# Order of causal masks, output evacuation and output tiles in a stick-breaking attention stage

## Chip, cores and metric

The kernel runs on 1 core of one Trainium2 chip. The metric is the device time of one execution in microseconds (us), median over several runs. The profile is of one further execution, recorded by the hardware.

## The reference

A trunk of two layers on a sequence of 512 tokens with 1024 features, in float32. Layer 0 mixes tokens with a gated linear recurrence, layer 1 with stick-breaking attention; each mixer is followed by a gated feed-forward block. The change lies in the attention of layer 1, 16 heads of width 64:

```
z = einsum(q, k) * scale                      # per head, scale = 1/8
mask = key_pos < q_pos
log_beta = log_sigmoid(z)
log_1m = where(mask, log_sigmoid(-z), 0)
suffix = cumsum(log_1m, reverse) - log_1m
wts = where(mask, exp(log_beta + suffix), 0)
out = einsum(wts, v);  x = x + out_all_heads @ w_out
```

## The kernel before

Scores are held transposed: 128 keys on the partitions, queries along the free dimension. There are four key tiles, kt = 0 to 3; only queries from the tile's own on count, so the tiles are 512, 384, 256 and 128 columns wide. One head takes three PSUM banks: kt 0 fills the first, kt 1 the second, kt 2 and 3 lie side by side in the third. Six banks hold two heads, so head h uses the banks of head h - 2. The other two banks take projections, outputs of heads and the first output tiles.

To keep float32 accuracy, every operand is split into a high and a low part (the names end in h and l); a product takes two or three matmuls. For a weight chunk of 128x1024 the high part is a cast on ScalarE (L306; on VectorE, L304, where `wh_dve` is set) and the low part a subtraction (L307) on VectorE or GpSimd (POOL).

The steps of a head h, with the lines of the profile:

- `s1(h)`: the score products (L1139 with the high part of q, L1140 with the low part), for kt 0 to 3, and the causal masks (L1142): a bf16 identity times a bf16 matrix of -1e30, added into the diagonal 128 columns. The mask of the first bank follows kt 0; those of the second and third bank follow kt 3 (the third is 256 columns wide, since it covers the diagonals of kt 2 and kt 3).
- `chain_a(h)`: for each bank, on ScalarE Abs (L1159), Exp (L1160) and Ln (L1161), on VectorE two softplus results (L1162, and L1163 as sph), on POOL the low part spl (L1164).
- `rsum(h)`: sums of the third bank on VectorE (L1172, L1175, L1177), called between the steps of `chain_b` of the head before.
- `s2(h)`: sixteen matmuls (L1196) that add the suffix sums into the score banks.
- `chain_b(h)`: for each bank, on ScalarE two exponentials (L1209 into awh, L1210 in place), on VectorE the low part of the weights, awl (L1211). After the last awl of head h its banks are free for `s1(h + 2)`.
- `s3(h)`: eight matmuls (L1222) with v. `s3_evac(h)`: a copy on ScalarE (L1235) and an addition on VectorE (L1236) that bring the head's output from PSUM to `o`. In the last heads (h >= 13) only one bank is left for `s3`, because another, `fill`, holds an output tile; so `s3` of the next head waits for `s3_evac` of the one before.

Beside these run the projections of q and k (`proj`, L352 to L354, evacuated by L1103, split by L1111, L1112 or L1124, L1125), three heads ahead, and from the sixth iteration on `osplit`, which splits finished pairs of heads (L1255, L1256) for the output projection. When the projections are used up, from iteration 13 on, `out_part(m, lo, hi)` fills TensorE's order with parts of the output tiles: the products of output tile m with the head pairs lo to hi - 1, three matmuls each. `out_split` splits the next output weight chunk ahead of time, with the cast on VectorE (L304). `out_add` (L1271) adds an output tile to x.

The order is written out by hand: the whole loop stands in `manual_schedule` for TensorE, ScalarE, VectorE and POOL, so each of these engines executes in program order and waits where an operand isn't ready. In iteration h the order is: first half of a projection (or an output part), `s1(h + 1)`, the first two banks of `chain_a(h + 1)`, `osplit`, the second half of the projection, the third bank of `chain_a(h + 1)`, `s3(h - 1)`, `s2(h)`, `chain_b(h)`, `out_split` (iterations 13 and 14), `s3_evac(h - 1)`.

Of the kernel before, what the change touches and what calls it, by code (L numbers as in the profile page):

```python
# [16 lines left out]
P = 128  # L17
# [23 lines left out]
def ts(i, n=P):  # L41
    return slice(i * n, (i + 1) * n)
# [128 lines left out]
class Kern:  # L171
# [858 lines left out]
    def attention(self):  # L1030
        nc, tc = self.nc, self.tc
        mm = nc.tensor.matmul
# [3 lines left out]
        with ExitStack() as cx:  # L1036
# [9 lines left out]
            idb = ap_.tile([P, P], BF16, name="idb")  # L1046
            msk = ap_.tile([P, 2 * P], BF16, name="msk")
# [17 lines left out]
            def mps():  # L1065
                self.mi += 1
                return mb[self.mi % len(mb)]
# [25 lines left out]
            def proj(t, part):  # L1093
                if part == 0:
                    self.pt = mps()
                    self.pw = self.chunk()
                wh, wl = self.pw
                for k in range(4 * part, 4 * part + 4):
                    self.mm3(self.pt, wh[:, ts(k)], wl[:, ts(k)], *self.u[k], k == 0, k == KT - 1)

            def proj_evac1(t):
                tt = self.tt = self.tmp()
                nc.vector.scalar_tensor_tensor(tt, self.pt, 1.0 if t % 2 else 0.125, self.rsB, ALU.mult, ALU.mult)  # L1103
# [24 lines left out]
            def zslot(h):  # L1128
                b = zb[3 * (h % 2):3 * (h % 2) + 3]
                return tuple(b[min(k, 2)][:, ZO[k]:ZO[k] + ZW[k]] for k in range(4)), b  # L1130

            def s1(h):
                hd = heads[h]
                zt, b = zslot(h)
                masks = {0: ((0, 0, P),), 3: ((1, 0, P), (2, P, 3 * P))}
                for kt in range(4):
                    qs = slice(QO[kt], S)
                    lk = hd["ks"][:, ts(kt)]
                    mm(zt[kt], lhsT=lk, rhs=hd["qh"][:, qs], start=kt < 3, stop=False, skip_group_check=True)  # L1139
                    mm(zt[kt], lhsT=lk, rhs=hd["ql"][:, qs], start=False, stop=False, skip_group_check=True)  # L1140
                    for i, lo, hi in masks.get(kt, ()):
                        mm(b[i][:, lo:hi], lhsT=idb, rhs=msk[:, :hi - lo], start=False, stop=True,  # L1142
                           skip_group_check=True)
                self.rel(hd["qh"], hd["ql"], hd["ks"])

            BR = (slice(0, 512), slice(0, 384), slice(128, 512))
# [68 lines left out]
            def s3(h):  # L1215
                hd = heads.pop(h)
                av = avs[h] = mps()
                for j, src in enumerate((hd["wh"], hd["wl"])):
                    for kt in range(4):
                        i, off = min(kt, 2), ZO[kt]  # L1220
                        w = ZW[kt]
                        mm(av[:, QO[kt]:QO[kt] + w], lhsT=vs[kt][h // 4][:, h % 4, :], rhs=src[i][:, off:off + w],  # L1222
                           start=kt == 0 and j == 0, stop=kt == 3 and j == 1, skip_group_check=True)
                self.rel(*hd["wh"], *hd["wl"])
                if h % 4 == 3:
                    self.rel(*(vs[t][h // 4] for t in range(NT)))
                if h % 2 == 0:
                    o[h // 2] = self.new("o")
# [3 lines left out]
            def s3_evac(h):  # L1232
                av = avs.pop(h)
                tt = self.tmp()
                nc.scalar.copy(tt[0:64], av[64:128])  # L1235
                nc.vector.tensor_tensor(o[h // 2][64 * (h % 2):64 * (h % 2) + 64], av[0:64], tt[0:64], ALU.add)  # L1236

            E = mybir.EngineType
            with tc.manual_schedule(engines={E.PE, E.Activation, E.DVE, E.Pool}):
                self.wl_dve = True  # L1240
                for t in range(3):
                    proj(t, 0)
                    if t == 2:
                        s1(0)
                        chain_a(0)
                        for i in range(3):
                            rsum(0, i)
                    proj(t, 1)
                    proj_evac1(t)
                    proj_evac2(t)  # L1250
                self.wl_dve = False
                def osplit(p):
                    oh, ol = ou[p] = self.new("oh", F32R, True), self.new("ol", F32R, True)
                    self.keep2 = max(0, self.keep2 - 2)
                    nc.scalar.copy(oh, o[p])  # L1255
                    nc.vector.tensor_tensor(ol, o[p], oh.bitcast(F32), ALU.subtract)  # L1256
                    self.rel(o[p])

                outs = {}

                def out_part(m, lo, hi, bank=None, stop=KT):
                    if m not in outs:
                        outs[m] = [None, *self.chunk(1 if m < 3 else None), 0]
                    e = outs[m]
                    if bank is not None:
                        e[0], e[3] = bank, lo
                    for k in range(lo, hi):
                        self.mm3(e[0], e[1][:, ts(k)], e[2][:, ts(k)], *ou[k], k == e[3], k == stop - 1)

                def out_add(m):  # L1270
                    nc.vector.tensor_tensor(self.x[m], self.x[m], outs[m][0], ALU.add)  # L1271

                def out_evac(m):
                    out_add(m)
                    outs.pop(m)
                    self.ffn_in(m, "g_ffn1")

                def out_split():
                    self.wh_dve = True
                    self.split_one()  # L1280
                    self.wh_dve = False

                nsp = 0
                due = None
                for h in range(NH + 1):
                    t = h + 3
                    if t < 16:
                        proj(t, 0)
                        if h == 1:
                            proj(t, 1)  # L1290
                            proj_evac1(t)
                    elif h == 13:
                        fill = mps()
                        out_part(0, 0, 2, fill, 6)
                    elif h == 14:
                        out_part(0, 2, 6, None, 6)
                    elif h == 15:
                        osplit(6)
                        out_part(1, 0, 6, fill)
                    elif h == 16:  # L1300
                        out_part(2, 0, 5, self.bank[0])
                    if h + 1 < NH:
                        s1(h + 1)
                        if h == 14:
                            out_add(0)
                        chain_a(h + 1, (0, 1))
                    if due is not None:
                        osplit(due)
                        due = None
                    if t < 16 and h != 1:  # L1310
                        proj(t, 1)
                        proj_evac1(t)
                    if h + 1 < NH:
                        chain_a(h + 1, (2,))
                    if h >= 13:
                        mb[:] = [b_ for b_ in (self.bank[6], self.bank[7]) if b_ is not fill]
                    if 1 <= h and h != 15:
                        s3(h - 1)
                    if t < 16 and t % 2:
                        proj_evac2(t)  # L1320
                    if h == 12:
                        self.free_u()
                        self.rel(*self.qrel)
                    if h < NH:
                        s2(h)
                        chain_b(h)
                    if h == 15:
                        s3(h - 1)
                    if h in (13, 14):
                        out_split()  # L1330
                    if h >= 1:
                        s3_evac(h - 1)
                    if t < 16 and t % 2 == 0:
                        proj_evac2(t)
                    if 6 <= h < 14 and 2 * nsp + 1 < h:
                        due = nsp
                        nsp += 1
                osplit(7)
                out_part(2, 5, 7)
                out_part(1, 6, 7)  # L1340
                out_part(0, 6, 7, self.bank[1])
# [92 lines left out]
```

## Time and profile before

| What | us |
|---|---|
| median of 3 runs (lowest, highest) | 1106.41 (1105.98, 1107.37) |
| the profiled execution, its device time | 1106.96 |
| its span, from first to last instruction | 1105.3 |
| PE busy in the span | 1089.0 |
| VectorE (DVE) busy | 901.4 |
| ScalarE (ACT) busy | 709.8 |
| GpSimd (POOL) busy | 363.2 |

Times in the timeline are microseconds from the start of the span. The loop over the heads lies between about 555 and 735 us. A row of the timeline has the start, the duration, the engine, the line, the operation, output<-input, shapes, and in brackets the idle time ahead of it with what ended it. Matmuls are pipelined: a matmul's duration includes its way through the array, so the pace is read from start to start. PEld rows are weight loads.

### The profile page before, as it was taken

What the parts mean: (1) busy time and instruction counts of PE and PEld (TensorE: products, weight loads), DVE (VectorE), ACT (ScalarE), POOL (GpSimd) and SP (SyncE); (2) the same over time, 40 slices, a digit from 0 to 9 for tenths busy, and PEclk for the clock granted to TensorE, in tenths of its full rate; (3) what the DMA queues carried; (4) which work ended last, traced back from release to release, by engine and by line L of the source; (5) the groups of instructions that cost most, each with busy time, mean ns of one, the idle gap of its engine ahead of it and who ended that gap; (6) DMA issues with size and microseconds to landing.
All of it is one profiled execution on the core that took longest, in us unless ns stands there. A gap on an engine that the chain in (4) does not pass through costs nothing.

```text
span 1105.3 us, 14729 instructions
## 1 busy us (share of the span) xinstructions
PE 1089.0 (99%) x5249; PEld 907.2 (82%) x5249; DVE 901.4 (82%) x1259; ACT 709.8 (64%) x1084; POOL 363.2 (33%) x253
## 2 busy tenths in 40 slices
PE   9999999999999999999999999999999999999996
PEld 6888888878888888888888888788888888888885
DVE  6878887696988888986379898978669897978897
ACT  6598567565646464635479999967765555546454
POOL 2444242315151514205034445413232424151411
PEclk9999999999999999999999999999999999999998
DMA  8513339887676765342243433224987776665421
GB/s 282 178 57 100 120 108 215 189 193 191 156 199 156 204 159 184 78 152 95 67 124 96 119 92 95 61 93 136 212 180 209 158 197 164 165 193 116 151 65 76
DMA packets 48825, 159.87 MB, mean 145 GB/s; under 512 B 6000, under 2 KB 7280, under 8 KB 48752
## 3 DMA queue, kind: packets, MB, share of 16 engines
q1 hardware_dynamic: 36368, 113.84, 30.5%
q0 software_dynamic: 12384, 45.09, 23.5%
q8 instruction: 41, 0.67, 0.2%
q14 instruction: 32, 0.26, 0.1%
HBM read 148.43 MB, written 2.10 MB: 136 GB/s over the span
## 4 chain that ended last, share of the span: by engine, by line
PE 69%; DVE 10%; ACT 6%; issue 4%; DMA 2%; POOL 0%; DVEq 0%; POOLq 0%; ACTq 0%
PE bank L773 15%; PE bank L774 15%; PE bank L775 15%; PE bank L352 6%; PE bank L354 6%; PE bank L353 6%; DVE wl L307 3%; PE bank L1196 2%; DMA bu<-w_gu 2%; PE bank L1222 1%; DVE y L765 1%; ACT wh L306 1%; PE bank L780 1%; ACT t L1160 1%; ACT t L1159 1%
## 5 line engine op out<-in xcount | busy, mean ns | idle before, releaser
L306 ACT CAST wh<-raw 128x1024 fp32r<-128x1024 f32 (+1 forms) x142 | 143.0, 1012 | 94.5 <-PE bank L775 35.0
L307 DVE TENSOR_TENSOR wl<-raw,wh 128x1024 fp32r<-128x1024 f32 (+1 forms) x116 | 172.1, 1487 | 36.1 <-ACT wh L306 36.0
L773 PE MATMUL bank<-wh,ow 128*128 128x512 f32 (+1 forms) x480 | 179.5, 374 | 0.0
L775 PE MATMUL bank<-wh,ow 128*128 128x512 f32 (+1 forms) x480 | 178.4, 372 | 0.0
L774 PE MATMUL bank<-wl,ow 128*128 128x512 f32 (+1 forms) x480 | 178.3, 371 | 0.0
L92 POOL DMA_DIRECT2D bu<-w_gu x64 | 56.1, 876 | 270.2 <-DVE wl L307 97.5
L306 ACT CAST wh<-bu 128x1024 fp32r<-128x1024 f32 x66 | 69.4, 1053 | 65.8 <-PE bank L775 34.1
L307 DVE TENSOR_TENSOR wl<-bu,wh 128x1024 fp32r<-128x1024 f32 x66 | 81.4, 1250 | 31.8 <-ACT wh L306 30.9
L352 PE MATMUL bank<-uh,wh 128*128 128x512 f32 x256 | 102.5, 401 | 0.8 <-ACT uh L408 0.8
L775 PEld LDWEIGHTS bank<-wh,ow 128*128 128x128 f32 x480 | 90.4, 188 | 15.7
L773 PEld LDWEIGHTS bank<-wh,ow 128*128 128x128 f32 x480 | 90.4, 188 | 15.6 <-issue 0.2
L774 PEld LDWEIGHTS bank<-wl,ow 128*128 128x128 f32 x480 | 90.5, 188 | 15.4
L354 PE MATMUL bank<-uh,wl 128*128 128x512 f32 x256 | 100.2, 392 | 0.4 <-DVE wl L307 0.3
L353 PE MATMUL bank<-ul,wh 128*128 128x512 f32 x256 | 100.0, 391 | 0.3 <-DVE ul L409 0.3
L307 POOL TENSOR_TENSOR wl<-raw,wh 128x1024 fp32r<-128x1024 f32 (+1 forms) x28 | 64.2, 2294 | 97.4 <-ACT wh L306 86.3
L765 DVE TENSOR_TENSOR y<-y,bank 128x512 f32<-128x512 f32 x140 | 89.1, 679 | 2.4 <-PE bank L775 2.3
L773 PE MATMUL bank<-wh,hth 128*128 128x512 f32 x192 | 75.2, 392 | 1.0 <-DVE y L765 1.0
L774 PE MATMUL bank<-wl,hth 128*128 128x512 f32 x192 | 74.9, 390 | 0.0
L775 PE MATMUL bank<-wh,htl 128*128 128x512 f32 x192 | 74.8, 390 | 0.0
L307 DVE TENSOR_TENSOR wl<-bv,wh 128x1024 fp32r<-128x1024 f32 x44 | 58.4, 1336 | 13.4 <-ACT wh L306 13.3
L1164 POOL TENSOR_TENSOR spl<-t,sph 128x512 fp32r<-128x512 f32 (+1 forms) x32 | 39.1, 1245 | 84.0 <-DVE sph L1163 76.6
L306 ACT CAST wh<-bv 128x1024 fp32r<-128x1024 f32 x44 | 46.1, 1051 | 18.3 <-PE bank L775 9.1
(262 smaller groups left out, 2765.9 us busy)
## 6 DMA issues: line engine op xcount, KB each, us to landing
bu<-w_gu POOLq DMA_DIRECT2D x64, 512.0 KB, 5.9
raw<-w_gu SPq DMA_DIRECT2D x44, 512.0 KB, 3.9
raw<-w_dn SPq DMA_DIRECT2D x24, 512.0 KB, 5.4
bu<-w_gu SPq DMA_DIRECT2D x22, 512.0 KB, 4.3
bv<-w_gu SPq DMA_DIRECT2D x22, 512.0 KB, 4.3
bv<-w_gu POOLq DMA_DIRECT2D x22, 512.0 KB, 6.3
d<-w_dn SPq DMA_DIRECT2D x20, 512.0 KB, 3.4
raw<-w_qk SPq DMA_DIRECT2D x16, 512.0 KB, 3.4
```

The source lines that it names most:

```text
L92: kern.soon(lambda: kern.nc.gpsimd.dma_start(t, self.part(n), accum_op=ALU.add))
L306: self.nc.scalar.copy(wh[:, c], raw[:, c])
L307: self.wl_engine(i).tensor_tensor(wl[:, c], raw[:, c], wh[:, c].bitcast(F32), ALU.subtract)
L352: mm(out, lhsT=wh, rhs=xh, start=first, stop=False)
L353: mm(out, lhsT=wh, rhs=xl, start=False, stop=False)
L354: mm(out, lhsT=wl, rhs=xh, start=False, stop=last)
L765: add = lambda o, a, b: nc.vector.tensor_tensor(o, a, b, ALU.add)
L773: mm(out, lhsT=xh, rhs=wh, start=first, stop=False, skip_group_check=True)
L774: mm(out, lhsT=xh, rhs=wl, start=False, stop=False, skip_group_check=True)
L775: mm(out, lhsT=xl, rhs=wh, start=False, stop=last, skip_group_check=True)
L1164: nc.gpsimd.tensor_tensor(sl[:, w], sp[:, w], sh[:, w].bitcast(F32), ALU.subtract)
L1196: mm(zt[kt][:, o0:o0 + ZW[j]], lhsT=tri if j == kt else one_n, rhs=s_, start=False, stop=True, skip_group_check=True)
```

## The change

Three edits. First, in `s1`, all three masks are issued after the products of all four key tiles, in the order first, second, third bank. The instructions are the same; only the mask of the first bank moves. Second, in iterations 13 and 14 `s3_evac(h - 1)` is issued ahead of `out_split`. Third, output tile 0 is done in parts of three and three head pairs in iterations 13 and 14, instead of two and four.

```
             def s1(h):
                 hd = heads[h]
                 zt, b = zslot(h)
-                masks = {0: ((0, 0, P),), 3: ((1, 0, P), (2, P, 3 * P))}
                 for kt in range(4):
...
                     mm(zt[kt], lhsT=lk, rhs=hd["ql"][:, qs], start=False, stop=False, skip_group_check=True)
-                    for i, lo, hi in masks.get(kt, ()):
-                        mm(b[i][:, lo:hi], lhsT=idb, rhs=msk[:, :hi - lo], start=False, stop=True,
-                           skip_group_check=True)
+                for i, lo, hi in ((0, 0, P), (1, 0, P), (2, P, 3 * P)):
+                    mm(b[i][:, lo:hi], lhsT=idb, rhs=msk[:, :hi - lo], start=False, stop=True, skip_group_check=True)
...
                     elif h == 13:
                         fill = mps()
-                        out_part(0, 0, 2, fill, 6)
+                        out_part(0, 0, 3, fill, 6)
                     elif h == 14:
-                        out_part(0, 2, 6, None, 6)
+                        out_part(0, 3, 6, None, 6)
...
+                    if h >= 1:
+                        s3_evac(h - 1)
                     if h in (13, 14):
                         out_split()
-                    if h >= 1:
-                        s3_evac(h - 1)
```

## The prediction

> **What bounds the kernel now.** Three views of the profile were read in this order: the waits inside the attention stage (555 to 760 us), busy time by stretch, and the timeline of single heads with all engines in one list.
>
> The waits first; a row gives who waited for whom, microseconds in total, times and the longest.
>
> ```profile
> PEld bank L1139 <- DVE awl L1211: 5.1, 11, 0.9
> ACT t L1159 <- PE bank L1142: 0.5, 2, 0.3
> ```
>
> A head's first score product (L1139) is held by VectorE's subtraction awl (L1211) of the head two before it, whose score banks it overwrites. ScalarE's first step on new scores, the Abs of L1159, hardly ever waits for a mask (L1142): 0.5 us in all. Busy time by stretch says how much of TensorE's time those holds can be.
>
> ```profile
> 575.00:595.00 20.00, 18.86 (x104) 15.39 (x103) 19.91 (x32) 19.11 (x38) 9.43 (x8) 1.00 0.34 87
> ```
>
> The columns are the stretch, its length, then PE, PEld, DVE, ACT and POOL busy, granted clock, DMA. From 575 to 595 PE is busy 18.86 of 20 us while DVE has 19.91 and ACT 19.11: ScalarE and VectorE are as full as TensorE. The timeline of head 9's scores, whose follow-up work ends at head 10's scores, shows how the three hang together.
>
> ```profile
> 649.82 1.04 ACT L306 CAST wh<-raw 128x1024 fp32r<-128x1024 f32 x1
> 649.95 0.39 PE L1139 MATMUL bank<-qh,ks 128*128 128x512 f32 x1
> 650.41 0.23 PE L1142 MATMUL bank<-msk,idb 128*128 128x128 bf16 x1
> 650.45 0.42 PE L1139 MATMUL bank<-qh,ks 128*128 128x384 f32 x1
> 650.71 0.33 PE L1140 MATMUL bank<-ql,ks 128*128 128x384 f32 x1
> 650.88 0.28 PE L1139 MATMUL bank<-qh,ks 128*128 128x256 f32 x1
> 650.89 0.60 ACT L1159 ACTIVATE t<-bank 128x512 f32<-128x512 f32 x1
> 651.29 0.34 PE L1142 MATMUL bank<-msk,idb 128*128 128x128 bf16 x2
> 652.19 0.63 ACT L1161 ACTIVATE t<-t 128x512 f32<-128x512 f32 x1
> 652.91 0.69 DVE L1162 SCALAR_TENSOR_TENSOR t<-bank,t 128x512 f32<-128x512 f32 x1 [0.43 <-issue]
> ...
> 661.48 0.55 DVE L1211 TENSOR_TENSOR awl<-bank,awh 128x384 fp32r<-128x384 f32 x1
> ...
> 662.09 0.39 PE L1139 MATMUL bank<-qh,ks 128*128 128x256 f32 x1
> ```
>
> The mask of the first bank starts at 650.41. Abs does not wait for it: it starts at 650.89, when the weight cast before it (649.82 + 1.04 = 650.86) is out of the way. Abs, Exp and Ln follow one another; Ln ends at 652.82 and VectorE, idle for 0.43 us, starts L1162 at 652.91. From there VectorE has no gap over 0.15 us until the last awl of head 8 ends at 661.48 + 0.55 = 662.03, and 0.06 us later TensorE's third product of head 10 starts, at 662.09. So Abs of head 9 sets the time of head 10's scores, with no slack anywhere between.
>
> **The change part by part.**
>
> Masks, TensorE's side. Now one mask stands between the first and the second key tile. It takes 0.04 us (650.41 to 650.45), and the 384-wide product behind it 0.26 (650.45 to 650.71) where the next one of that width takes 0.17 (650.71 to 650.88): 0.13 us go. In exchange a third mask joins the two at the end.
>
> ```profile
> L1142 PE MATMUL bank<-msk,idb x48: 229/230/273, 557.2 to 714.3; 128*128 128x128 bf16 x32, 128*128 128x256 bf16 x16
> ```
>
> The longest, 0.27 us, is the 256-wide one; the late pair lasts 0.34 in all (651.29), so it starts 0.07 after its neighbour, and a third mask costs about 0.07. Net 0.06 us saved a head, 1.0 us over 16, where TensorE sets the pace. The Trainium skill (TensorE: Matmul & The Clock Gate, section Back-to-back issue gap) puts a stream of 128-column matmuls with their weight loads at about 81 ns each; by that a third mask would cost 0.08 and 0.8 us would be saved; the measured spacing is taken.
>
> Masks, ScalarE's side: the term that counts. The first bank is complete only when its mask has run, and that mask will stand behind all eight products. In head 9 it moves from 650.41 to 651.29 - 0.13 = 651.16. How soon Abs can follow a mask is read where it did wait for one, in head 0.
>
> ```profile
> 557.25 0.23 PE L1142 MATMUL bank<-msk,idb 128*128 128x128 bf16 x1
> 557.52 0.60 ACT L1159 ACTIVATE t<-bank 128x512 f32<-128x512 f32 x1 [0.18 <-PE bank L1142]
> 558.13 0.34 PE L1142 MATMUL bank<-msk,idb 128*128 128x128 bf16 x2
> ...
> 565.94 0.62 ACT L1111 CAST qx<-t 128x512 fp32r<-128x512 f32 x1 [3.51 <-DVE t L1103]
> ```
>
> It is 0.27 us from start to start. So Abs of head 9 moves to 651.43, 0.54 later than 650.89. Queued behind the waiting Abs on ScalarE are its Exp and Ln, both other banks, and the exponentials of head 8 (chain_b); VectorE waits for them, and TensorE's third product of head 10 for VectorE: it moves by the same 0.54. The third mask behind it makes 0.61 for heads 9 and 10. Of the heads 5, 7, 9, 11 and 13 the first and the last stand here beside head 9 (0.94 from first product to Abs in head 5 and in head 9, 0.95 in head 13):
>
> ```profile
> 607.39 0.39 PE L1139 MATMUL bank<-qh,ks 128*128 128x512 f32 x1
> 608.33 0.60 ACT L1159 ACTIVATE t<-bank 128x512 f32<-128x512 f32 x1
> ...
> 618.15 0.55 DVE L1211 TENSOR_TENSOR awl<-bank,awh 128x384 fp32r<-128x384 f32 x1
> 618.96 0.28 PE L1139 MATMUL bank<-qh,ks 128*128 128x256 f32 x1
> ...
> 693.84 0.39 PE L1139 MATMUL bank<-qh,ks 128*128 128x512 f32 x1
> 694.79 0.60 ACT L1159 ACTIVATE t<-bank 128x512 f32<-128x512 f32 x1
> ```
>
> Heads 9, 11 and 13 carry the output splits (osplit) of both engines, and heads 10, 12 and 14 are held: 3 x 0.61 = 1.83 us. Heads 3, 5 and 7 leave a little slack, read from head 5: the awl ends at 618.70 and could release at 618.76, the product of head 6 starts at 618.96, 0.20 later. 0.34 of the 0.54 is left, the restart after a stall costs 0.11 (the 256-wide product lasts 0.39 at 662.09, 0.28 at 650.88) and the third mask 0.07: 0.5 a pair, 1.5 us. In the even heads Abs comes later too, but the work that it delays has more time before the next odd head; I count nothing.
>
> Head 0: Abs moves from 557.52 to 558.13 - 0.13 + 0.27 = 558.27, 0.75 later. VectorE does head 0's chain ahead of L1103, for which ScalarE waits 3.51 us (565.94) before its casts, Abs of head 1, and so awl of head 0, which holds head 2. No slack shows: 0.75 in full; the other end is nothing, should a queue catch it up.
>
> ```profile
> 577.45 0.59 ACT L1159 ACTIVATE t<-bank 128x512 f32<-128x512 f32 x1
> 577.84 0.39 PE L1139 MATMUL bank<-qh,ks 128*128 128x256 f32 x1
> 578.36 0.34 PE L1142 MATMUL bank<-msk,idb 128*128 128x128 bf16 x2
> ...
> 582.74 0.59 ACT L1210 ACTIVATE bank<-bank 128x512 f32<-128x512 f32 x1
> 583.93 0.68 DVE L1211 TENSOR_TENSOR awl<-bank,awh 128x512 fp32r<-128x512 f32 x1
> ```
>
> Head 2 is held itself: its first mask runs before the held products, and Abs starts at 577.45, ahead of the third product (577.84). Afterwards it comes at 578.36 + 0.27 = 578.63, 1.18 later. The exponential that awl of head 1 reads ends at 583.33, and VectorE comes to it at 583.93; with 0.06 to hand over, 0.54 of the 1.18 is covered, and head 3 moves by 0.64.
>
> The last heads.
>
> ```profile
> 703.75 0.50 PE L1139 MATMUL bank<-qh,ks 128*128 128x512 f32 x1 [0.48 <-DVE awl L1211]
> 704.59 0.60 ACT L1159 ACTIVATE t<-bank 128x512 f32<-128x512 f32 x1
> 705.21 0.39 PE L1139 MATMUL bank<-qh,ks 128*128 128x256 f32 x1
> ...
> 713.11 0.54 DVE L1211 TENSOR_TENSOR awl<-bank,awh 128x384 fp32r<-128x384 f32 x1
> 713.71 0.39 PE L1139 MATMUL bank<-qh,ks 128*128 128x256 f32 x1
> 713.91 0.68 DVE L304 CAST wh<-raw 128x1024 fp32r<-128x1024 f32 x1
> 714.51 0.67 DVE L1236 TENSOR_TENSOR o<-bank,t 64x512 f32<-64x512 f32 x1
> 714.67 2.41 POOL L307 TENSOR_TENSOR wl<-raw,wh 128x1024 fp32r<-128x1024 f32 x1 [2.43 <-DVE wh L304]
> 715.24 0.50 PE L1222 MATMUL bank<-awh,vs 128*128 128x512 f32 x1 [0.67 <-DVE o L1236]
> ```
>
> Head 14 is held like head 2: Abs at 704.59 comes 0.62 ahead of the third product (705.21) and will come 0.52 + 0.27 = 0.79 behind it (0.52 from 577.84 to 578.36), 1.41 later. Head 15's third product (713.71) follows the awl of head 13 (713.11 + 0.54 = 713.65) at once, so it loses all 1.41; the 0.07 behind head 14, counted above, does not delay it: 1.34.
>
> Equal parts: three more products of 0.23 us (0.46 from 649.95 to 650.41 for two), 0.69 in all, go ahead of head 14's scores, into the 0.48 us wait, and leave the place ahead of head 15's scores. Both places end at a wait for awl, so nothing is won: 0. If the second place were not held it would give back up to 0.69.
>
> Evacuation first: L1236 comes 0.60 earlier (713.91 in place of 714.51), and the product that waits for it (715.24): -0.60. The cast L304 comes 0.60 later, and behind it POOL's half of the split, done at 717.08 now; its first reader stands 24 matmuls (s3, s2) behind 715.24, so it costs 0, or up to 0.60 without them. In the next head the same swap meets no waiting product: 0.
>
> Sum: 0.75 + 0.64 + 1.5 + 1.83 + 1.34 - 0.60 = 5.46. The 0.06 a head is not taken off, since every second head is held by VectorE and not by TensorE. The profiled execution took 1106.96 us (span 1105.3); with 5.5 it gives 1112.5. It lies 0.55 above the median of the runs, 1106.41, and on that scale the forecast is **1111.9 us**.
>
> **The rivals.** (1) TensorE sets the pace and the others catch up, so that the edits give what they save on TensorE: 1.0 + 0.60 + 0.48 = 2.1 us, some 0.4 more with restarts that vanish, 1103.9. For it: PE is busy 18.86 of 20 us even in the worst stretch. It decides if VectorE had 0.5 us of slack between Ln and awl; against it, 0.06 us from 662.03 to 662.09. Chance 0.07. (2) The delay counts only where the loop is tight, heads 9, 11 and 13, and the ends catch it up: 1.83 - 0.60 = 1.2, 1107.6. For it: the slack in head 5, and that TensorE saves 0.06 a head. Chance 0.10. (3) The stalls cost clock as well: twelve 512-wide products of a half projection at half clock would take 2.8 us more, and in the seven held heads 20 us: 1132. Against it, the stretch 575 to 595 with 1.14 us of idle TensorE has a granted clock of 1.00. Chance 0.01. The Trainium skill (the same page, section A second HAM failure mode: psum-queue depth-cycling) warns that frequent short idles between groups of matmuls can make the clock gate close and open; that row does not agree. (4) Abs is not released by its own mask but by the last of the three, 0.14 later: ten heads make 1.4 more, 1113.3. This lies within my forecast.
>
> **How the numbers follow.** The forecast, (4) included, has 0.82. Its low end: head 0 and head 2 caught up (-1.4) and half of head 15 (-0.7), 1109.8; its high end, (4) and a restart of 0.11 in each of 16 heads (1.8): 1115. The range reaches down into rival 2, to 1108.2. About 0.2% (2.2 us) is what can be told from no change: faster 0.07, the same 0.10 (rival 2), slower 0.83.
>
> **What would show it.** In the profile of the changed kernel Abs (L1159) should wait for the mask in nearly every head, some 0.3 to 0.6 us each, where two waits stood; VectorE's idle before L1162 should grow by as much; TensorE should wait for awl in all even heads from 4 on and longest in head 15; and the wait for L1236 ahead of L1222 in the last heads should shrink. If Abs waits but awl is no later against the scores, the chain has slack that I did not see, and rival 2 or 1 holds; if the heads from 4 to 8 show no wait, the 1.5 is wrong.

## The result and the profile after

| What | before | after |
|---|---|---|
| median of 6 runs each, us (lowest, highest) | 1106.01 (1105.15, 1107.37) | 1112.70 (1111.47, 1115.09) |
| ratio after/before, 95% interval | | 1.0060 (1.0049 to 1.0071) |
| the profiled execution, device time (span) | 1106.96 (1105.3) | 1111.47 (1109.8) |

The change makes the kernel slower by 5.4 to 7.9 us (the interval of the ratio times 1106). The lines of the code after have moved up by one or two: the score products are L1138 and L1139, the masks L1141, Abs, Exp and Ln L1157 to L1159, the softplus results L1160 and L1161, awl L1209, the products with v L1220, the evacuation L1233 and L1234.

The two profiled executions differ by 4.51 us, the medians by 6.7. The first score product of head 0 shows a part of the reason (timeline, before, then after):

```profile
556.79 0.39 PE L1139 MATMUL bank<-qh,ks 128*128 128x512 f32 x1
```

```profile
555.91 0.39 PE L1138 MATMUL bank<-qh,ks 128*128 128x512 f32 x1
557.12 0.39 PE L1141 MATMUL bank<-msk,idb 128*128 128x128 bf16 x3
557.39 0.60 ACT L1157 ACTIVATE t<-bank 128x512 f32<-128x512 f32 x1 [0.93 <-PE bank L1141]
```

What lies ahead of that product is the same code in both, and took 0.88 us less in the execution recorded after. In the profiles of this study it took from 555.59 to 558.51 us, and the part from the end of attention to the end of the program, the same code again, from 341.04 to 343.61. That is the scatter of a us or two between runs of one kernel. So all shifts below are counted from head 0's first score product and end at the first product of the feed-forward block (L773): 764.03 - 556.79 = 207.24 before, 768.73 - 555.91 = 212.82 after. The attention stage is 5.6 us longer, and 4.51 + 0.88 = 5.39 is what the whole execution lost from there on. The about 1 us more between the medians is of the size of that scatter; no run here says what makes it.

The waits inside the attention stage (555 to 760 us), after; the columns are microseconds, times, longest:

```profile
PEld bank L1138 <- DVE awl L1209: 15.3, 25, 1.6
DVE t L1160 <- ACT t L1159: 12.3, 16, 1.8
ACT t L1157 <- PE bank L1141: 9.8, 14, 1.5
DVE t L1160 <- POOL wl L307: 5.4, 3, 1.8
...
DVE t L1160 <- issue: 1.8, 4, 0.5
```

and VectorE's two rows ahead of its first step on new scores, before:

```profile
DVE t L1162 <- issue: 8.4, 9, 1.4
DVE t L1162 <- ACT t L1161: 3.9, 9, 0.9
```

Abs waits for the mask 14 times and 9.8 us, where it was twice and 0.5 us. One engine on, VectorE stands idle ahead of that step (which waits for Ln) for 12.3 + 5.4 + 1.8 = 19.5 us in place of 8.4 + 3.9 = 12.3, some 0.5 a head more; the releaser that a row names differs, the place is the same. At the end of a head's work TensorE's weight loads wait for awl, 15.3 us in place of 5.1. ScalarE waits 9.3 us more, and head 15's scores come 6.0 us later (next section); the rest fell into slack. Busy time by stretch, after:

```profile
575.00:595.00 20.00, 17.85 (x99) 14.52 (x99) 18.89 (x32) 18.21 (x36) 8.71 (x7) 1.00 0.33 84
```

PE, DVE and ACT are each some 0.9 to 1.0 us less busy than before in the same 20 us: no engine took the time, all three wait for one another. Over the whole stage, 555 to 760 us, PE is busy 199.1 us in place of 202.3, DVE 174.1 in place of 178.3, ACT 174.6 in place of 179.2. The granted clock stays at 1.00. The timeline of head 9 and of the third product of head 10, after:

```profile
651.88 1.05 ACT L306 CAST wh<-raw 128x1024 fp32r<-128x1024 f32 x1
651.93 0.39 PE L1138 MATMUL bank<-qh,ks 128*128 128x512 f32 x1
653.14 0.39 PE L1141 MATMUL bank<-msk,idb 128*128 128x128 bf16 x3
653.41 0.60 ACT L1157 ACTIVATE t<-bank 128x512 f32<-128x512 f32 x1 [0.49 <-PE bank L1141]
654.71 0.63 ACT L1159 ACTIVATE t<-t 128x512 f32<-128x512 f32 x1
655.43 0.69 DVE L1160 SCALAR_TENSOR_TENSOR t<-bank,t 128x512 f32<-128x512 f32 x1 [0.48 <-issue]
664.00 0.55 DVE L1209 TENSOR_TENSOR awl<-bank,awh 128x384 fp32r<-128x384 f32 x1
664.61 0.39 PE L1138 MATMUL bank<-qh,ks 128*128 128x256 f32 x1
```

The cast is over at 652.93 and ScalarE stands idle until the mask; Abs starts 653.41 - 651.93 = 1.48 us behind the head's first product (0.94 before), 0.27 behind the first of the masks. At the far end the awl of head 8 ends at 664.55 and the product starts 0.06 later, as before: the chain is unchanged, and Abs, which starts it, comes 0.54 us later.

### The profile page after: what moved, and what is told of

Same layout as the page of the kernel before. It is cut to its first block, busy times and chain, and to the rows that moved or that the text cites. A ratio compares the mean times of both kernels' runs of the same rounds, so it can differ in the third digit from the quotient of the medians.

```text
span 1109.8 us, 14729 instructions
## 1 busy us (share of the span) xinstructions
PE 1091.7 (98%) x5249; PEld 908.3 (82%) x5249; DVE 901.8 (81%) x1259; ACT 709.5 (64%) x1084; POOL 363.2 (33%) x253
## 4 chain that ended last, share of the span: by engine, by line
PE 75%; DVE 10%; ACT 3%; issue 3%; POOL 0%; DVEq 0%
PE bank L773 17%; PE bank L774 17%; PE bank L775 17%; PE bank L352 6%; PE bank L354 6%; PE bank L353 6%; DVE wl L307 3%; PE bank L1194 2%; DVE y L765 1%; PE bank L780 1%; PE bank L1220 1%; ACT t L1158 1%; ACT t L1157 1%; DVE awl L1209 1%; PE bank L1138 1%
## 5 line engine op out<-in xcount | busy, mean ns | idle before, releaser
L307 DVE TENSOR_TENSOR wl<-raw,wh 128x1024 fp32r<-128x1024 f32 (+1 forms) x116 | 171.7, 1481 | 36.9 <-ACT wh L306 36.7
L773 PE MATMUL bank<-wh,ow 128*128 128x512 f32 (+1 forms) x480 | 179.5, 374 | 0.0
L775 PE MATMUL bank<-wh,ow 128*128 128x512 f32 (+1 forms) x480 | 178.3, 372 | 0.0
L774 PE MATMUL bank<-wl,ow 128*128 128x512 f32 (+1 forms) x480 | 178.3, 371 | 0.0
L307 DVE TENSOR_TENSOR wl<-bu,wh 128x1024 fp32r<-128x1024 f32 x66 | 82.5, 1266 | 29.6 <-ACT wh L306 28.8
L773 PEld LDWEIGHTS bank<-wh,ow 128*128 128x128 f32 x480 | 90.4, 188 | 15.4
L307 POOL TENSOR_TENSOR wl<-raw,wh 128x1024 fp32r<-128x1024 f32 (+1 forms) x28 | 64.0, 2288 | 97.4 <-ACT wh L306 85.7
L773 PE MATMUL bank<-wh,hth 128*128 128x512 f32 x192 | 75.2, 392 | 0.9 <-DVE y L765 0.9
L307 DVE TENSOR_TENSOR wl<-bv,wh 128x1024 fp32r<-128x1024 f32 x44 | 58.4, 1336 | 13.2 <-ACT wh L306 13.1
L352 PEld LDWEIGHTS bank<-uh,wh 128*128 128x128 f32 x256 | 48.6, 190 | 11.2 <-ACT wh L306 1.7
```

What stands on the lines that cost most here:

```text
L307: self.wl_engine(i).tensor_tensor(wl[:, c], raw[:, c], wh[:, c].bitcast(F32), ALU.subtract)
L352: mm(out, lhsT=wh, rhs=xh, start=first, stop=False)
L773: mm(out, lhsT=xh, rhs=wh, start=first, stop=False, skip_group_check=True)
L774: mm(out, lhsT=xh, rhs=wl, start=False, stop=False, skip_group_check=True)
L775: mm(out, lhsT=xl, rhs=wh, start=False, stop=last, skip_group_check=True)
```

## Where the time went, head by head

The shift of a head is the start of its third score product, counted from head 0's first, minus the same before. For head 10: (664.61 - 555.91) - (662.09 - 556.79) = 3.40. The last two columns are the first product with v of head 13, which runs behind head 15's scores, and the feed-forward block. The rows below the first are the experiments that follow; one profiled execution each.

| us later than before, at | 2 | 3 | 4 | 6 | 8 | 10 | 12 | 14 | 15 | v of 13 | feed-forward |
|---|---|---|---|---|---|---|---|---|---|---|---|
| after | 0.74 | 1.08 | 1.71 | 2.21 | 2.71 | 3.40 | 4.00 | 4.59 | 5.97 | 5.37 | 5.59 |
| masks alone | 0.74 | 1.30 | 1.91 | 2.39 | 2.88 | 3.57 | 4.14 | 4.76 | 6.14 | 6.14 | 6.93 |
| evacuation alone | -0.01 | -0.84 | -0.22 | -0.12 | -0.12 | -0.12 | -0.11 | -0.12 | -0.13 | -0.73 | -0.71 |
| equal parts alone | 0.00 | 0.01 | 0.03 | -0.01 | -0.01 | 0.00 | -0.01 | -0.02 | -0.03 | -0.03 | -0.04 |
| odd heads 3 to 13 | 0.00 | 0.01 | 0.50 | 0.96 | 1.40 | 2.04 | 2.58 | 3.12 | 3.11 | 3.10 | 3.14 |
| heads 1 and 4 to 12 even | -0.01 | -0.85 | -0.23 | -0.23 | -0.30 | -0.16 | -0.04 | 0.09 | 0.07 | 0.07 | 0.07 |
| a copy ahead of Abs | -0.02 | -0.85 | 0.29 | 0.71 | 1.12 | 1.73 | 2.25 | 2.78 | 2.77 | 2.77 | 2.83 |
| mask behind kt 1 | 0.34 | -0.04 | 0.57 | 0.60 | 0.62 | 0.85 | 1.00 | 1.11 | 1.79 | 1.79 | 1.85 |

In several rows head 3 is about 0.85 earlier, of which 0.12 is left from head 6 on. That belongs to no edit; the last section tells where it comes from.

## The experiments

The theory: Abs of the odd heads is on a chain ScalarE, VectorE, TensorE without slack, so what delays Abs delays the kernel. The first rival: TensorE's order sets the pace, and the late masks cost through TensorE or through all heads alike. The second: the cost is one of the other two edits.

**The three edits one by one.** Masks alone is the first hunk of the change, evacuation alone the swap of `out_split` and `s3_evac`, equal parts alone the two `out_part` calls.

> The kernel before with the first edit alone: all three masks behind a head's eight score products. My theory (the later first mask delays Abs on ScalarE, and through VectorE's awl the score products two heads on): the whole cost of the change and the 0.6 us that the evacuation wins back on top, so about 6.1 us slower than before, some 1112.5 us; head 15's third product 5.9 to 6.1 us later against head 0's first product than before. Rival (TensorE sets the pace; the cost of the change comes from the edits in the last heads): 1.0 us faster than before, since 16 switches between data types are saved.

> The kernel before with the second edit alone (output evacuation ahead of the weight split in iterations 13 and 14). My theory: the wait of the first s3 product of head 13 shrinks by 0.60 us and all behind it comes 0.6 earlier; that is under what the runs can tell, so it is read in the trace, from head 0's first score product on. Rival (the moved weight split is read in time no more, or the saving is lost at the next wait): 0 or later.

> The kernel before with the third edit alone (output tile 0 in parts of three and three head pairs). My theory: the 0.48 us wait ahead of head 14's scores fills up, but head 15's third score product comes no earlier, within 0.1 us, since it is released by VectorE: 0. Rival (what TensorE saves at head 14 stays saved): 0.5 us earlier from head 15 on.

Masks alone: 1113.47 us beside 1106.73 before, ratio 1.0062 (1.0047 to 1.0077). Evacuation alone: 1106.74 beside 1106.69, 0.9995 (0.9984 to 1.0005); equal parts alone: 1105.95, 0.9994 (0.9985 to 1.0003). The masks carry the whole loss. The swap does gain, but too little to show in the times of whole runs: in its row the shift goes from -0.13 at head 15 to -0.73 at the next products, 0.60 us. In the timeline of that kernel the evacuation stands ahead of the cast, and the products with v follow it:

```profile
712.24 0.41 DVE L1177 TENSOR_TENSOR r<-t,r 128x256 fp32r<-128x256 f32 x1
712.58 0.68 DVE L1236 TENSOR_TENSOR o<-bank,t 64x512 f32<-64x512 f32 x1
713.18 0.68 DVE L304 CAST wh<-raw 128x1024 fp32r<-128x1024 f32 x1
713.30 0.86 PE L1222 MATMUL bank<-awh,vs 128*128 128x512 f32 x4
```

With equal parts alone the wait ahead of head 14's scores is filled, and the one ahead of head 15's, where the products were taken from, opens:

```profile
702.55 0.40 PE L354 MATMUL bank<-oh,wl 128*128 128x512 f32 x1
702.79 0.43 PE L1139 MATMUL bank<-qh,ks 128*128 128x512 f32 x1
...
712.01 0.45 PE L1139 MATMUL bank<-qh,ks 128*128 128x384 f32 x1 [0.28 <-DVE awl L1211]
712.08 0.55 DVE L1211 TENSOR_TENSOR awl<-bank,awh 128x384 fp32r<-128x384 f32 x1
712.68 0.39 PE L1139 MATMUL bank<-qh,ks 128*128 128x256 f32 x1
```

The third product of head 15 still starts 0.05 us behind the end of awl (712.63): what the wait was worth in the one place it costs in the other.

Masks alone also shows a term that no single edit had: from head 15's scores on it loses 0.79 us more (6.14 to 6.93). Masks alone, timeline of the last iterations:

```profile
730.44 0.68 DVE L304 CAST wh<-raw 128x1024 fp32r<-128x1024 f32 x1
731.15 1.23 DVE L307 TENSOR_TENSOR wl<-raw,wh 128x1024 fp32r<-128x1024 f32 x1
732.41 0.69 DVE L1234 TENSOR_TENSOR o<-bank,t 64x512 f32<-64x512 f32 x1
733.15 0.86 PE L1220 MATMUL bank<-awh,vs 128*128 128x512 f32 x4 [0.55 <-DVE o L1234]
```

With Abs of head 15 late as well, the evacuation one iteration later, behind both halves of a weight split, is the last to arrive, and the products of head 14 with v wait 0.55 us for it. With the swap the same products do not wait (after, timeline):

```profile
728.54 0.68 DVE L1234 TENSOR_TENSOR o<-bank,t 64x512 f32<-64x512 f32 x1
729.25 0.70 DVE L304 CAST wh<-raw 128x1024 fp32r<-128x1024 f32 x1
...
730.01 0.80 PE L1220 MATMUL bank<-awh,vs 128*128 128x512 f32 x4
```

So beside the late masks the swap is worth 0.6 us in one iteration and about 0.55 in the next. The second is most of what masks alone lost beyond the 6.1 us expected of it (6.93 in the stage). After the change 0.22 us more are still lost behind head 15 (5.37 to 5.59): 0.16 of it is a wait of the suffix products (L1194, at 728.56) for VectorE's r (L1175).

**Only the odd heads, only the even ones.**

```
-                masks = {0: ((0, 0, P),), 3: ((1, 0, P), (2, P, 3 * P))}
+                last = h in (3, 5, 7, 9, 11, 13)
+                masks = {3: ((0, 0, P), (1, 0, P), (2, P, 3 * P))} if last else {0: ((0, 0, P),), 3: ((1, 0, P), (2, P, 3 * P))}
```

The even kernel has (1, 4, 6, 8, 10, 12) in this place.

> All masks at the end only in heads 3, 5, 7, 9, 11 and 13, elsewhere as before; the other half of the heads that had the masks late in the even heads. My theory: the pair terms alone, 3 x 0.5 and 3 x 0.55 to 0.61, 3.0 to 3.3 us slower than before, as with the copy put ahead of Abs. Rival (the cost grows with the number of late masks, wherever they are): as little as with the even heads, 0.

> All masks at the end only in heads 1, 4, 6, 8, 10 and 12; in the odd heads from 3 on and in heads 0, 2 and 14 as before. My theory: Abs of these heads waits too, but the awl that it delays has 0.9 us or more before the next odd head's scores, so the time stays within 0.7 us of before, rather faster (0.06 us a head). Rival (every late mask costs its own delay): 5 times 0.5 us, 2.5 us slower.

Odd heads: 1109.78 beside 1107.0, ratio 1.0025 (1.0016 to 1.0035), 3.14 us in the attention stage. Heads 1 and 4 to 12 even: 1106.79 beside 1106.73, 1.0002 (0.9993 to 1.0011). Six heads each; the one set costs 3 us, the other nothing that a run can tell. It is not that Abs of the even heads would not wait (waits, the even kernel, where Abs is L1160, the masks L1143 and the scores L1140):

```profile
ACT t L1160 <- PE bank L1143: 2.8, 7, 0.5
...
PEld bank L1140 <- DVE awl L1212: 6.8, 15, 1.0
```

2.8 us of waiting for masks (0.5 before) hardly reaches the scores: most of the work that this Abs delays has time before the next odd head. It isn't quite nothing. Against evacuation alone, which has the same kind of start, head 15 comes 0.2 us later (0.07 and -0.13): 0.18 us is gained up to head 8, and each of the three tight pairs (9-10, 11-12, 13-14) loses 0.12 to 0.14, as TensorE's longer wait for awl (6.8 us, 5.1 before) shows too. Abs of heads 9, 11 and 13 comes 1.00 to 1.03 us behind the first product there, 0.07 to 0.09 later than before. The first rival, a price at every head alike, falls; what matters is which head waits, not how long ScalarE waits in all.

**The same delay without any mask.** The masks stay where they were; a copy that is dead work, since Abs overwrites what it writes, delays Abs of the odd heads on ScalarE itself.

```
+                    if i == 0 and h in (3, 5, 7, 9, 11, 13):
+                        nc.scalar.copy(e, self.rsB)
                     nc.scalar.activation(e[:, w], z, AF.Abs)
```

> The kernel before, masks where they were, with one more copy of 128x512 (its result is overwritten at once) on ScalarE ahead of Abs in heads 3, 5, 7, 9, 11 and 13: about 0.55 us, as much as the later mask costs there, with TensorE's order untouched. My theory: heads 10, 12 and 14 come 0.55 us later each, heads 4, 6 and 8 some 0.45 each (0.2 of slack, 0.11 for the restart), about 3.0 us slower in all. Rival (the cost lies in TensorE's order of masks, or ScalarE has slack): within 0.5 us of before.

1109.94 beside 1106.73, ratio 1.0034 (1.0018 to 1.005). The timeline of head 9 there, with TensorE's stream as before and the copy in Abs's place:

```profile
652.24 0.39 PE L1139 MATMUL bank<-qh,ks 128*128 128x512 f32 x1
652.74 0.42 PE L1139 MATMUL bank<-qh,ks 128*128 128x384 f32 x1
653.05 0.61 ACT L1160 COPY t<-acc 128x512 f32<-128x512 f32 x1
653.70 0.60 ACT L1161 ACTIVATE t<-bank 128x512 f32<-128x512 f32 x1
...
664.30 0.55 DVE L1213 TENSOR_TENSOR awl<-bank,awh 128x384 fp32r<-128x384 f32 x1
664.90 0.39 PE L1139 MATMUL bank<-qh,ks 128*128 128x256 f32 x1
```

Abs starts 1.46 behind the head's first product, within 0.02 of the changed kernel, and the tight pairs lose 0.61, 0.52 and 0.53 us, the changed kernel 0.69, 0.60 and 0.59. The odd-head kernel, with the same Abs delayed by its mask, loses 0.64, 0.54 and 0.54, that is 0.01 to 0.03 more than the copy. So it is Abs's delay that costs, and not the new order on TensorE in these heads; the other 0.05 to 0.06 of the changed kernel comes with the late masks of the even heads, where a third mask stands behind the held products.

**A quarter of the delay.**

```
-                masks = {0: ((0, 0, P),), 3: ((1, 0, P), (2, P, 3 * P))}
+                masks = {1: ((0, 0, P),), 3: ((1, 0, P), (2, P, 3 * P))}
```

> A smaller dose: the first bank's mask stands behind the products of the second key tile, the other two at the end as before. Its start moves by 0.34 us in place of 0.75. My theory: Abs comes 0.13 us later in the odd heads, which counts in heads 9, 11 and 13 only (0.4 us), 0.34 later in head 0, and 0.7 later in head 14, which head 15 pays: about 1.4 us slower than before. Rival A (a cost of having the masks apart from the start of the chain at all, not of their lateness): as much as the full edit, 6 us. Rival B (three masks in a row at the end are what costs): no change.

1109.68 beside 1106.73, ratio 1.0027 (1.0015 to 1.0038), 1.85 us in the attention stage. Abs of the odd heads comes 0.13 us later (1.07 behind the first product), and the tight pairs lose 0.23, 0.15 and 0.11; heads 4 to 8, with their 0.2 us of slack, lose 0.05 together. Head 0 pays 0.34 and head 15 0.68. The total is 0.45 more than the 1.4 expected. Half of that, 0.23, appears between heads 2 and 4: ScalarE stands idle 0.36 us for head 2's mask there, a term that the expectation didn't have. How the rest splits was not traced. The cost follows the delay of Abs, and the slack of the loop is seen from both sides: 0.13 us vanishes in it, 0.54 does not.

**The chain shortened.** If the chain is the bound, work taken out of it must pay. Two things lay in it without need: the output split's cast L1255 between ScalarE's steps for the second and the third bank of heads 9 and 11, and head 0's third bank on VectorE ahead of L1103, for which ScalarE waited 3.51 us. The first kernel has the change's swap of the evacuation, and osplit of iterations 8 and 10 behind `chain_b`:

```
-                    if due is not None:
+                    if due is not None and (h % 2 or h > 12):
                         osplit(due)
                         due = None
...
                         chain_b(h)
+                        if due is not None:
+                            osplit(due)
+                            due = None
```

The second has in the prologue, for t == 2:

```
-                        chain_a(0)
-                        for i in range(3):
-                            rsum(0, i)
+                        chain_a(0, (0, 1))
                     proj(t, 1)
                     proj_evac1(t)
+                    if t == 2:
+                        chain_a(0, (2,))
                     proj_evac2(t)
+                    if t == 2:
+                        for i in range(3):
+                            rsum(0, i)
```

> The kernel before with the evacuation first, and with the two output splits of iterations 8 and 10 moved behind the exponentials and awl of that iteration (0.8 us of VectorE and 0.5 us of ScalarE leave the path from Abs of heads 9 and 11 to the scores of heads 10 and 12). My theory that this path sets the pace there: heads 10 and 12 come some 0.6 us earlier each, with the evacuation 1.8 us faster in all. Rival (the moved work is in the way of the next Abs): no gain beyond 0.6.

> The kernel before with the start of the loop reordered: head 0's third bank and its sums come behind the evacuation of the third projection, not ahead of it. The 3.51 us that ScalarE waits for L1103 shrink, Abs of head 1 and awl of head 0 come 2 us or more earlier. My theory (head 0's chain holds heads 2 and 3): the waits at head 2 (1.2 us) go, and of those at head 3 (1.1 us) a part: 1.2 to 2.0 us faster. Rival (head 0's chain has slack, so that the 0.75 us counted for it in the prediction was no real term): no change.

The osplit kernel: 1104.69 beside 1106.69, ratio 0.9986 (0.9975 to 0.9996), 1.83 us off the attention stage, as expected (1.8). The prologue kernel: 1105.78, ratio 0.9992 (0.9982 to 1.0002), 1.05 us off it, a gain that the trace shows and the runs can't tell from nothing. The prologue's timeline:

```profile
561.15 0.68 DVE L1103 SCALAR_TENSOR_TENSOR t<-bank,acc 128x512 f32<-128x512 f32 x1
561.86 0.63 ACT L1111 CAST qx<-t 128x512 fp32r<-128x512 f32 x1 [0.19 <-DVE t L1103]
```

The wait of 3.51 is 0.19, and Abs of head 1 comes 2.84 us earlier, but head 2's scores only 1.05: the last awl of head 0 now ends 1.6 us before they start, so that TensorE's own stream is the next bound, and the expected 1.2 to 2.0 was not quite reached. The start told in the last section has, by the row of evacuation alone, 0.12 us of the gain in each of these kernels, and the swap 0.60 in the first: its osplit is worth about 1.1, the prologue about 0.9. Two kernels put this together. The first joins both and also moves iteration 13's osplit to iteration 14, so that the head pair it splits joins output tile 0 in its last part; the second joins both and leaves iteration 13 alone.

> A version against the chain that the runs so far show: masks as before, evacuation first, head 0's third bank behind the third projection's evacuation, output splits of iterations 8 and 10 behind awl, and the split of iteration 13 moved into iteration 14 (its head pair joins the last part of output tile 0). Of head 0's first score product: -1.05 (prologue), -1.86 (splits, evacuation), and up to -0.8 more at head 15, whose awl loses the split ahead of it: 3 to 3.8 us faster than before, some 1103 us. Rival (the waits moved elsewhere): not below the 1104.7 of the splits alone.

> The version before it without the move of iteration 13's output split, which put 0.69 us of products behind head 15 where nothing covers them: masks as before, evacuation first, prologue reordered, splits of iterations 8 and 10 behind awl. From head 0's first score product to the feed-forward block: -1.05 and -1.83, 2.8 to 2.9 us less than before, some 1103.5 to 1104 us. Rival (the two gains cover one another): 1.8 us at most.

With the move: 1105.04 beside 1107.0, ratio 0.9977 (0.9965 to 0.9988). It gains 3.26 us up to head 13's products with v, and gives 0.68 of them back behind head 15, where the three products moved (0.69 us) now run: 2.58 is left, less than the 3 to 3.8 expected. Without the move: 1104.83 beside 1107.42, ratio 0.9978 (0.9968 to 0.9988), and 2.75 us off the attention stage (2.8 to 2.9 expected: 1.05 + 1.83 counts the start's 0.12 us twice). Both beat the kernel before and the changed one, as the osplit kernel alone does; the two can't be told apart by the runs, whose medians, some 1105, are above the 1103 to 1104 expected.

## Why the prediction was right

The forecast was 1111.9 us, the median is 1112.7, inside the range, and by the mechanism it named: late masks delay Abs, and Abs delays the scores through VectorE's awl. That the sum fits to 0.1 us is in part luck, since a term that came out 0.30 too large stands against others that came out 0.2 too small. The medians of the runs differ by 6.7, 1.2 more than the 5.5 forecast, and the trace of the stage shows only 0.1 of that.

- **Abs 0.54 later in the tight heads**, from 0.27 us between a mask and Abs: measured 0.54 in head 9 (0.94 to 1.48), and 0.27 in head 0 and head 9. Abs is released by the first of the three masks: they start 0.06 us apart ((0.39 - 0.27) / 2 from the row of three and the longest mask alone, 0.27), so the last of them starts 0.12 later, and Abs would have come at 653.53 and not 653.41. The fourth rival is wrong.
- **Pairs 9-10, 11-12, 13-14**, 1.83: measured 0.69 + 0.60 + 0.59 = 1.88, of which 1.72 comes with the odd heads' masks (0.64 + 0.54 + 0.54). The pairs from 3 to 8, 1.5: measured 0.63 + 0.50 + 0.50 = 1.63, and awl ends 0.05 us ahead of the product in every even head from 4 on, as the prediction asked of them.
- **Head 0**, 0.75: measured 0.74. **Even heads**, nothing: 0.07 us for six of them against before, 0.2 against a kernel with the same kind of start.
- **Head 3**, 0.64: measured 0.34 (1.08 - 0.74). The mechanism was there: the first awl of head 1 comes 584.43 - 555.91 = 28.52 us behind head 0's start, against 583.93 - 556.79 = 27.14, 1.38 later, where 0.64 + 0.75 was said. What followed gave 0.3 of it back. Before, then after:

```profile
583.93 0.68 DVE L1211 TENSOR_TENSOR awl<-bank,awh 128x512 fp32r<-128x512 f32 x1
584.45 1.02 POOL L1164 TENSOR_TENSOR spl<-sp,sph 128x384 fp32r<-128x384 f32 x1
584.53 1.23 DVE L1172 TENSOR_TENSOR t<-sp 128x256 f32<-128x256 f32 x1
```

```profile
584.43 0.68 DVE L1209 TENSOR_TENSOR awl<-bank,awh 128x512 fp32r<-128x512 f32 x1
584.66 1.00 POOL L1162 TENSOR_TENSOR spl<-sp,sph 128x384 fp32r<-128x384 f32 x1 [0.29 <-DVE sph L1161]
585.03 0.92 DVE L1170 TENSOR_TENSOR t<-sp 128x256 f32<-128x256 f32 x1
```

Head 3's next awl stands behind VectorE's sum (L1172, L1170), and the sum ends 0.29 us behind POOL's spl in both (585.47 and 585.76, 585.66 and 585.95), as it does wherever the two meet with POOL ahead (last section). Before, spl started when POOL was through with the two ahead of it; after, POOL waits for sph, 0.29 us, so that its backlog had already taken up a part of the delay. Counted from head 0 the sum ends 30.04 us in, against 28.97: 1.07 later, and that is head 3's shift of 1.08. This is read from the two traces and was not tried by itself. Nor is the term a constant: masks alone shows 1.30 at head 3 where evacuation alone, with the same kind of start (last section), shows -0.84. How much head 2's late Abs costs by itself stays open.

- **Head 15**, 1.34: measured 1.38. **Equal parts**, 0: measured -0.04. **Evacuation**, -0.60: measured -0.60, alone and in the change.
- **What failed** is a sentence: "In the next head the same swap meets no waiting product: 0". It is true of the kernel before. With the masks late the product does wait, 0.55 us in masks alone, and the swap takes that away. The two cancel in the sum, so the total did not show it: what the prediction lacked was the cost of the late masks behind head 15, and the same gain of the swap. Edits were priced against the kernel before, not against each other.

Sum up to head 13's products with v: predicted 5.46, measured 5.37. One reading of the prediction was too simple: that VectorE is as full as TensorE from 575 to 595, busy 19.91 of 20 us. 3.1 us of that are waits inside two of its operations (2.65 and 1.23 us where they take 0.41 elsewhere; last section). No term of the sum rests on it. Rival 1 (TensorE sets the pace) needed 0.5 us of slack between Ln and awl, and the even heads have such slack, the odd ones not. Rival 2 (only heads 9, 11 and 13) fell with heads 0, 3 to 8 and 15, 4.1 us of the masks' 5.97. Rival 3 (the clock): the stretch from 575 to 595 has 2.15 us of idle TensorE in place of 1.14, the whole stage 5.9 in place of 2.7, and both a clock of 1.00.

## What to carry to other kernels

When several engines are each busy for nearly nine tenths of a loop or more (here TensorE 202, VectorE 178, ScalarE 179 of 205 us), the bound can be a chain that runs through them: look for a stretch in which each step starts as soon as the one before it ends, from engine to engine (here from Abs of an odd head to the scores of the next head), and price an edit by how far it moves the start of that chain, not by the work it saves on the busiest engine. A result that another engine waits for is worth issuing as soon as its inputs are there, even in the middle of a stream of large products: here an edit that saves some 0.06 us a head on TensorE cost 0.5 to 0.7 in every second head. And price the edits of one change against each other as well: one can take away the slack that made another worthless.

## What the runs showed of the hardware

A 0.41 us operation of VectorE took 2.65 us in some executions, where it meets a weight split on POOL. The timeline before, then of evacuation alone, where the code up to here is the same:

```profile
577.67 2.40 POOL L307 TENSOR_TENSOR wl<-raw,wh 128x1024 fp32r<-128x1024 f32 x1 [2.62 <-ACT wh L306]
577.71 2.65 DVE L1177 TENSOR_TENSOR r<-t,r 128x256 fp32r<-128x256 f32 x1
```

```profile
576.47 2.70 POOL L307 TENSOR_TENSOR wl<-raw,wh 128x1024 fp32r<-128x1024 f32 x1 [2.63 <-ACT wh L306]
576.50 0.41 DVE L1177 TENSOR_TENSOR r<-t,r 128x256 fp32r<-128x256 f32 x1
```

In neither do they run side by side: either POOL takes its 2.40 and VectorE ends 0.29 behind it, or VectorE takes its 0.41 and POOL is 0.30 longer. The Trainium skill (SBUF — State Buffer, section SBUF: two separate sides) says that VectorE and GpSimd share a pair of ports as an exclusive lock, which the one that starts first holds for the whole instruction. The trace agrees with the lock; which engine got it in these two rows is not to be read from the records, where POOL starts 0.03 us earlier in both. Where the starts lie further apart, the order agrees too. In the profile before, VectorE's sum L1172 meets POOL's spl (L1164) six times with POOL ahead by 0.07 us or more; there it takes 0.83 to 1.23 us and ends 0.28 behind POOL. Once it is ahead of POOL, and takes the usual 0.42; one meeting of each kind:

```profile
563.40 0.42 DVE L1172 TENSOR_TENSOR t<-sp 128x256 f32<-128x256 f32 x1
563.57 1.13 POOL L1164 TENSOR_TENSOR spl<-sp,sph 128x384 fp32r<-128x384 f32 x1 [0.45 <-DVE sph L1163]
...
647.37 1.02 POOL L1164 TENSOR_TENSOR spl<-sp,sph 128x384 fp32r<-128x384 f32 x1 [0.81 <-PE bank L1196]
647.85 0.83 DVE L1172 TENSOR_TENSOR t<-sp 128x256 f32<-128x256 f32 x1
```

Of the two orders of L307 and L1177, the one with POOL first was in the profiles of before, after, equal parts and the odd heads, the other in all the rest. In evacuation alone, with VectorE first, head 3 comes 0.84 us earlier and the heads from 6 on 0.12; the rows of the table that begin with about -0.85 at head 3 have the same start.
